# A two-layer hybrid decoder step: sums of squares, a group mean and modulation products regrouped on TensorE

## The chip, the cores and the metric

The kernel runs on one core of a Trainium2 chip. The metric is the device time of one execution in microseconds; lower is better. The traces are of single profiled executions.

## What is computed

Two decoder layers are applied to a prompt of 512 tokens and to 8 samples of 4 tokens (32 tokens), so activations are 1024 channels by 544 tokens. Cut to what the change touches:

```python
mod = silu(c) @ w_ada + b_ada            # 9 conditioning vectors, 1024 -> 6*1024
h   = rmsnorm(x, norm1) * (1 + sc1) + sh1
q   = rope(rmsnorm(q per head of 64, q_norm), pos)     # 16 heads
k   = rope(rmsnorm(k per head of 64, k_norm), pos)     # 4 heads
...
# state-space branch, 4 groups of 512 channels
y, hT = ssd_scan(xs, dt, A, B, C, h0)    # h0: one state of 512 x 128 per sample and group
yg = y * silu(z), in 4 groups
yg = yg * rsqrt(mean(yg * yg, over the group's 512 channels) + eps)
```

Everything is float32. The large projections are split in a high and a low float32r half of both operands, so one projection tile is three products.

## The kernel before

Channels lie on partitions, tokens on the free axis: an activation of 1024 channels is 8 tiles of 128x544. `gemm` (L336) multiplies one weight block of 1024x128 with the 8 tiles of `h`: 8 x 3 weights x 2 halves of 272 tokens, 48 products, of which the trace mostly shows rows of two (x2). A weight block comes by DMA on SP's queue into `raw` (four buffers, L318), ScalarE makes its high half `wh` (L177), VectorE its low half `wl` (L322), with three buffers of each.

Side work is written as Python generators in four lanes. Each `gemm` first advances each lane by its rate (`pump`). Lane "c" holds the state-space chains, in the order in which they are pushed, lane "a" the modulation, lanes "s" and "t" the indexer's scores and its top-k. A scheduler in the compiler then sorts each engine's instructions by priorities and by times of its own; the order is fixed before the run, and each engine takes its instructions strictly in that order.

The places that the change touches:

- **Modulation** (`ada`). A call makes 16 blocks of 128 columns. Per call there are four accumulators, each 128x512, and four loads of `raw` (128x1024, L250) per accumulator. Each load feeds two products (L253): 32 columns of stationary conditioning vectors, 512 moving columns. A product writes one of four bands of 32 partitions: the first and third load write bands 0 and 1, the second and fourth write bands 2 and 3. There is a `yield` behind each load, so a `gemm` stands between two loads' products. Six calls in all: the first in the prologue, two during layer 0's pooling and attention, three during layer 0's feed-forward part.
- **Sums of squares** (`ssq`, L483), for 8 query tiles and 2 key tiles per layer. The squared tile is the stationary operand, in five blocks of tokens; two columns of 1/64 are the moving one. The rsqrt is three Newton steps on VectorE (L271 to L276) on 128x80 (queries) or 128x20 (keys).
- **The state-space mean** (`norm_rows`), once per group, 8 in all. Five products with one column (L284) put the mean with tokens on partitions, Newton runs on 128x5 elements, five products with the identity (L295, L297) spread the result over all partitions, and ScalarE copies it to `rb`. L1137 multiplies `Y` by `rb`; `oh` and `ol` (L310) are its halves, which the next product of the branch takes (L336, `psg<-oh,wh`).
- **States of the samples** (`ssd_sample`). Per group, 8 states `h0` (128x512; the trace strips the digit and says `h`) are loaded four at a time (L1084), and a `yield` later each is multiplied by 32 columns of `cm` into one of four bands (L1088).

In float32 the trace shows two records for a product of TensorE (a float32r product and a transpose have one). L740 (`kx`, indexer keys of the samples) is another product in four bands of 32.

## Time and profile before

| | |
|---|---|
| median of 3 runs | 3217.64 us (3216.38 to 3218.22) |
| profiled execution: time, span | 3219.4 us, 3217.6 us |
| busy in the span: TensorE, VectorE, ScalarE, GpSimd | 3117.6 (97%), 2229.4 (69%), 1258.1 (39%), 892.9 us (28%) |
| mean granted clock of TensorE | 0.985 of full speed |

The time of an execution is the span from the first to the last recorded instruction and 1.8 us around it. Busy time of TensorE counts overlapping products once. In the views below a row of the timeline is one or more equal instructions in a row, with its start and its length; the distance from its start to the next row's start is what it took on an engine that is never idle.

### The profile page before, as it was taken

To read this page: it belongs to the slowest core of one execution; us is meant where nothing else is said; L and a number is where in the kernel's file an instruction comes from. 1 tells how busy PE (TensorE), PEld (TensorE's weight loads), DVE (VectorE), ACT (ScalarE), POOL (GpSimd) and SP (SyncE) were. 2 spreads that over 40 slices of the span, in tenths; PEclk is the share of its full clock that TensorE was granted. 3 is DMA by queue.
4 is the path that set the end of the run, shared out by engine and by line. 5 is a ranking of instruction groups with operands and counts; after the bars stand their busy time and mean duration, and the time that the engine had idled before them with its cause. 6 is when DMAs were issued, how large, how long until landed. Compare 5 with 4: busy or idle time off the path is not lost. (4 is left out here: it accounts for less than half of the span.)

```text
span 3217.6 us, 63012 instructions
## 1 busy us (share of the span) xinstructions
PE 3117.6 (97%) x24322; PEld 2834.3 (88%) x24322; DVE 2229.4 (69%) x4827; ACT 1258.1 (39%) x2228; POOL 892.9 (28%) x1271
## 2 busy tenths in 40 slices
PE   7999999999999999999999999999999999999999
PEld 5987898999896788888989978989999967899999
DVE  5687788679878655444566877886799976564554
ACT  4344443333236534333443444433342365352432
POOL 2373445421021002111223544455120210030211
PEclk8999999999999999999999999999999999999999
DMA  6332332345433434445334323233233234333322
GB/s 231 104 104 77 110 95 101 105 151 179 164 117 129 157 133 115 147 146 147 105 104 122 98 82 106 89 96 119 95 129 117 91 125 154 106 84 94 78 98 78
DMA packets 303102, 376.85 MB, mean 117 GB/s; under 512 B 177362, under 2 KB 186930, under 8 KB 302802
## 3 DMA queue, kind: packets, MB, share of 16 engines
q1 hardware_dynamic: 116514, 315.94, 29.3%
q10 hardware_dynamic: 181216, 42.05, 6.4%
q0 software_dynamic: 5072, 14.83, 1.2%
q8 instruction: 192, 3.15, 0.4%
q14 instruction: 108, 0.88, 0.1%
HBM read 330.34 MB, written 33.79 MB: 113 GB/s over the span
## 5 line engine op out<-in xcount | busy, mean ns | idle before, releaser
L177 ACT ACTIVATE wh<-raw 128x1024 fp32r<-128x1024 f32 (+2 forms) x434 | 424.9, 980 | 1199.7 <-PE psg L336 909.6
L336 PE MATMUL psg<-hh,wh 128*128 128x272 f32 x4064 | 863.7, 292 | 7.8 <-ACT cacc L839 5.4
L336 PE MATMUL psg<-hl,wh 128*128 128x272 f32 x4064 | 856.0, 290 | 0.0
L336 PE MATMUL psg<-hh,wl 128*128 128x272 f32 x4064 | 853.6, 290 | 0.0
L322 DVE TENSOR_TENSOR wl<-raw,wh 128x1024 fp32r<-128x1024 f32 (+2 forms) x434 | 510.5, 1176 | 354.1 <-ACT wh L177 349.8
L336 PEld LDWEIGHTS psg<-hh,wh 128*128 128x128 f32 x4064 | 642.6, 189 | 61.9 <-issue 28.1
L336 PEld LDWEIGHTS psg<-hh,wl 128*128 128x128 f32 x4064 | 643.9, 189 | 17.1 <-issue 15.3
L336 PEld LDWEIGHTS psg<-hl,wh 128*128 128x128 f32 x4064 | 644.1, 189 | 15.9 <-issue 14.4
L841 POOL COPY sti<-cu 128x32 f32<-128x32 f32 x136 | 91.3, 672 | 588.9 <-ACT cu L177 588.6
L846 DVE SCALAR_TENSOR_TENSOR cacc<-cu,half,cacc 128x511 f32<-128x511 f32 x144 | 134.9, 937 | 6.8 <-ACT cacc L839 6.3
L336 PE MATMUL psg<-fh,wh 128*128 128x272 f32 x648 | 135.4, 291 | 2.6 <-DVE resid L460 2.6
L855 ACT ACTIVATE th<-cacc 128x544 f32<-128x544 f32 x92 | 60.5, 657 | 196.1 <-DVE cacc L849 187.5
L454 DVE SCALAR_TENSOR_TENSOR x<-psg,mod,x 128x272 f32<-128x272 f32 x64 | 32.0, 500 | 151.6 <-PE psg L336 142.6
L336 PE MATMUL psg<-fl,wh 128*128 128x272 f32 x648 | 133.7, 287 | 0.0
L336 PE MATMUL psg<-fh,wl 128*128 128x272 f32 x648 | 133.7, 288 | 0.0
L336 PEld LDWEIGHTS psg<-fh,wh 128*128 128x128 f32 x648 | 101.2, 188 | 14.3 <-issue 6.7
L336 PE MATMUL psg<-oh,wh 128*128 128x272 f32 x512 | 110.4, 294 | 0.0
L336 PE MATMUL psg<-ol,wh 128*128 128x272 f32 x512 | 109.5, 291 | 0.0
L336 PE MATMUL psg<-oh,wl 128*128 128x272 f32 x512 | 109.0, 292 | 0.0
L856 DVE SCALAR_TENSOR_TENSOR cacc<-th,cacc 128x544 f32<-128x544 f32 x92 | 71.3, 775 | 49.2 <-ACT th L855 49.0
L986 POOL TENSOR_TENSOR seg<-seg,cb 128x512 f32<-128x512 f32 x64 | 88.9, 1392 | 54.3 <-ACT seg L985 46.8
L336 PEld LDWEIGHTS psg<-fl,wh 128*128 128x128 f32 x648 | 101.7, 188 | 0.0
(469 smaller groups left out, 6232.4 us busy)
## 6 DMA issues: line engine op xcount, KB each, us to landing
raw<-wk SPq DMA_DIRECT2D x326, 512.0 KB, 3.5
raw<-w_ada SPq DMA_DIRECT2D x96, 512.0 KB, 3.5
h<-h SPq DMA_DIRECT2D x64, 256.0 KB, 3.8
raw<-wk SPq DMA_DIRECT2D x64, 256.0 KB, 2.8
o_ssds<-hn ACTq DMA_DIRECT2D x64, 256.0 KB, 2.2
raw<-wd SPq DMA_DIRECT2D x32, 448.0 KB, 3.4
kvr<-ckv SPq DMA_DIRECT2D x48, 256.0 KB, 3.6
kvw<-ckv SPq DMA_DIRECT2D x48, 256.0 KB, 4.0
```

Of the source, the lines that this page charges most:

```text
L177: self.nc.scalar.activation(out, src, AF.Copy)
L322: self.last_wl = self.E("weights1").tensor_tensor(wl[:, :n], raw[:, :n], wh[:, :n].bitcast(F32), op=OP.subtract).ins
L336: nc.tensor.matmul(o[:, c, :HC], w[:, k * 128:(k + 1) * 128], x[:, c * HC:(c + 1) * HC], start=(k == 0 and first), stop=(k == K - 1 and last))
L454: self.E("resid1").scalar_tensor_tensor(x[:, :HC], o[:, 0, :HC], g[:, 0:1], x[:, :HC], op0=OP.mult, op1=OP.add)
L841: self.E("conv1").tensor_copy(st[:, i, :, W - 1:], new)
L846: self.E("conv3").scalar_tensor_tensor(acc[:, s:512], u[:, :512 - s], wc, acc[:, s:512], op0=OP.mult, op1=OP.add)
L855: nc.scalar.activation(th, acc, AF.Tanh)
L856: self.E("silu21").scalar_tensor_tensor(acc, th, 1.0, acc, op0=OP.add, op1=OP.mult)
L986: self.E("ssd_chain5").tensor_tensor(d[:, :512], d[:, :512], cb[:, :512], op=OP.mult)
```

## The change

Four edits.

- **Modulation.** The loads are taken in pairs: the first of a pair is followed by a `yield`, then both loads' four products are written back to back, one in each band.
- **Sums of squares.** A block of 128x32 (`blk32`, the two columns of 1/64 and 30 of zeros) is now stationary and the squared tile moves (512 and 32 columns). Four query tiles, or two key tiles, go to four (two) bands. ScalarE copies the bands out, TensorE transposes them back. The Newton steps of the queries run per four tiles on 128x40. `qsq` leaves the tag "R" (one buffer) for "T" (49 buffers).
- **The state-space mean.** One 128x128 stationary block of 1/512 gives the mean on all partitions (512 and 32 moving columns). The Newton steps run on 128x544. The five products with the identity and the copies to `rb` are gone.
- **States of the samples.** The first four loads of `h0` stand at the head of `ssd_sample`, the second four behind the first four products, and the `yield` between loads and products is gone.

```diff
 def ada(...):
         for c in range(4):
             ps = self.P("ada1")
-            for z in range(4):
-                i = 4 * c + z
-                with self.tc.high_priority(offset=WPRI):
-                    raw = self.wr.tile([128, 1024], F32, name="raw", tag="raw")
-                    nc.sync.dma_start(raw, a["w_ada"][l, s, i])
-                for q in range(2):
-                    k, g = 2 * z + q, 32 * (2 * (z % 2) + q)
-                    nc.tensor.matmul(ps[g:g + 32, :], self.sc[:, k, :], raw[:, q * 512:(q + 1) * 512],
-                                     start=(k < 4), stop=(k >= 4))
-                if z < 3:
+            for pair in range(2):
+                raws = []
+                for z in (2 * pair, 2 * pair + 1):
+                    with self.tc.high_priority(offset=WPRI):
+                        raw = self.wr.tile([128, 1024], F32, name="raw", tag="raw")
+                        nc.sync.dma_start(raw, a["w_ada"][l, s, 4 * c + z])
+                    raws.append(raw)
+                    if z % 2 == 0:
+                        yield
+
+                for k4 in range(4):
+                    nc.tensor.matmul(ps[32 * k4:32 * k4 + 32, :], self.sc[:, 4 * pair + k4, :],
+                                     raws[k4 // 2][:, (k4 % 2) * 512:(k4 % 2) * 512 + 512],
+                                     start=(pair == 0), stop=(pair == 1))
+                if pair == 0:
                     yield
...
 def norm_rows(self, sq, wcol, eps, out):
-        ps = self.P("norm_rows1")
-        for i in range(5):
-            w = 128 if i < 4 else 32
-            nc.tensor.matmul(ps[:w, i:i + 1], sq[:, i * 128:i * 128 + w], self.mean_w[:, wcol:wcol + 1],
-                             start=True, stop=True)
...
+        o, o2 = self.P("norm_rows1"), self.P("norm_rows2")
+        nc.tensor.matmul(o, self.mean512, sq[:, :512], start=True, stop=True)
+        nc.tensor.matmul(o2[:, :32], self.mean512, sq[:, 512:], start=True, stop=True)
+        m, u, y = self.t("nrm"), self.t("nru"), self.t("rb")
+        nc.vector.tensor_scalar(m[:, :512], o, eps, None, op0=OP.add)
+        nc.vector.tensor_scalar(m[:, 512:], o2[:, :32], eps, None, op0=OP.add)
+        yield
+        self.newton(m, u, y)
+        out.append(y)
         yield
...
-    def ssq(self, sq, ps, c0):
-        for i in range(5):
-            w = 128 if i < 4 else 32
-            self.nc.tensor.matmul(ps[:w, i * 16 + c0:i * 16 + c0 + 2], sq[:, i * 128:i * 128 + w], self.blk,
-                                  start=True, stop=True)
+    def ssq(self, sqs, name):
+
+        nc, n = self.nc, len(sqs)
+        o, o2 = self.P("ssq3"), self.P("ssq4")
+        for z, sq in enumerate(sqs):
+            nc.tensor.matmul(o[32 * z:32 * z + 32, :], self.blk32, sq[:, :512], start=True, stop=True)
+        for z, sq in enumerate(sqs):
+            nc.tensor.matmul(o2[32 * z:32 * z + 32, :32], self.blk32, sq[:, 512:], start=True, stop=True)
+        rows = self.t("ssr")
+        self.copy("ssq1", rows[:32 * n, :512], o[:32 * n])
+        self.copy("ssq1", rows[:32 * n, 512:], o2[:32 * n, :32])
...
+        for i in range(4):
+            nc.tensor.transpose(ps[:, 128 * i:128 * i + 32 * n], rows[:32 * n, 128 * i:128 * i + 128],
+                                self.ident[:32 * n, :32 * n])
...
 def ssd_sample(self, q):
+        def states(hf):
+            h0s = [self.t("h0") for z in range(4)]
+            for z in range(4):
+                nc.sync.dma_start(h0s[z][:, :512], a["h0"][l, g, 4 * hf + z])
+            return h0s
+        nxt = states(0)
...
-            h0s = [self.t("h0") for z in range(4)]
-            for z in range(4):
-                nc.sync.dma_start(h0s[z][:, :512], a["h0"][l, g, 4 * hf + z])
-            yield
+            h0s = nxt
             for z in range(4):
...
-            if hf:
+            if not hf:
+                nxt = states(1)
+            else:
...
 def attention(self):
         for i in range(8):
...
-            self.ssq(sq, ps, 2 * i)
+            sqs.append(sq)
+            if i % 4 == 3:
+                mk = self.ssq(sqs, "mq")
+                self.newton(mk, self.s([128, 5, 8], "rsq_u8"), rq[:, :, 2 * i - 6:2 * i + 2])
+                sqs = []
```

What the diff alone does not show is how the scheduler places the products. A row below is a line, an operation, output and inputs, the output's shape and a count; the lines after L216 are shifted in the changed program (gemm L336 is L339, modulation L253 is L263, states L1088 is L1109, `kx` L740 is L757).

On TensorE in layer 0's feed-forward part, before: two loads (`raw_15524`, `raw_15593`) with one gemm (output `psg_15534`) between them.

```order
L253 MATMUL psb_15523<-raw_15524,sc_101 32x512 x2
L336 MATMUL psg_15534<-hh_14969,wh_15530 128x272 x2
L336 MATMUL psg_15534<-hl_14977,wh_15530 128x272 x2
...
L336 MATMUL psg_15534<-hh_14976,wl_15531 128x272 x2
L253 MATMUL psb_15523<-raw_15593,sc_101 32x512 x2
L336 MATMUL psg_15603<-hh_14969,wh_15599 128x272 x2
```

The same place in the changed program:

```order
L339 MATMUL psg_15505<-hh_14949,wl_15502 128x272 x2
L263 MATMUL psb_15496<-raw_15497,sc_106 32x512 x2
L263 MATMUL psb_15496<-raw_15564,sc_106 32x512 x2
L339 MATMUL psg_15576<-hh_14942,wh_15572 128x272 x2
...
L339 MATMUL psg_15651<-hh_14949,wl_15648 128x272 x2
L263 MATMUL psb_15496<-raw_15643,sc_106 32x512 x2
L263 MATMUL psb_15496<-raw_15710,sc_106 32x512 x2
```

Two loads' products now stand together, with two gemms to the next four. Counted over the program without the prologue (its 32 products stand as before), the 160 modulation products stood in 71 uninterrupted runs (61 of two, 7 of four, one each of one, three and six) and now stand in 44 (35 of four, 5 of two, 2 of one, one each of three and five).

On TensorE in layer 0's first state-space group, before: the second four states of the samples (`h0_2731` to `h0_2734`).

```order
L1088 MATMUL psa_2606<-h0_2731,cm_2603 32x512
L745 MATMUL psb_2636<-rel_2634,wsel_1588 32x512
L336 MATMUL psg_3005<-hh_145,wl_3002 128x272 x2
L1088 MATMUL psa_2606<-h0_2732,cm_2603 32x512
L336 MATMUL psg_3005<-hh_146,wh_3001 128x272 x2
L336 MATMUL psg_3005<-hl_154,wh_3001 128x272 x2
L336 MATMUL psg_3005<-hh_146,wl_3002 128x272
L1088 MATMUL psa_2606<-h0_2733,cm_2603 32x512
```

The same group in the changed program (`h0_2494` on are the first four, `h0_2633` on the second):

```order
L1109 MATMUL psa_2624<-h0_2494,cm_2621 32x512
L1091 MATMUL psb_2612<-smt_2525,sxdt_2507 64x32 x8
L1109 MATMUL psa_2624<-h0_2495,cm_2621 32x512
L1109 MATMUL psa_2624<-h0_2496,cm_2621 32x512
L1109 MATMUL psa_2624<-h0_2497,cm_2621 32x512
...
L1109 MATMUL psa_2624<-h0_2633,cm_2621 32x512
L1109 MATMUL psa_2624<-h0_2634,cm_2621 32x512
L1109 MATMUL psa_2624<-h0_2635,cm_2621 32x512
L1109 MATMUL psa_2624<-h0_2636,cm_2621 32x512
```

The states that stood one by one between gemm products now stand together. Over the program, the 64 state products stood in 40 runs (30 of one, 6 of three, 4 of four) and now stand in 18 (4 of one, 4 of three, 8 of four, 2 of eight); the 32 products of L740 go from 10 runs to 8 of four. The 20 sums of squares of 512 columns do not all stand together: 10 stand alone and 10 in 5 pairs, each as soon as its tile is there, so 15 runs, and the 20 of 32 columns likewise, mostly right behind them.

On VectorE in layer 0's second state-space group the changed program has, from the mean (`nrm`) to the product with `Y` (the Newton steps are L286 to L291, L325 makes `wl`):

```order
L301 TENSOR_SCALAR nrm<-psa 128x512
L302 TENSOR_SCALAR nrm<-psa 128x32
L795 TENSOR_TENSOR qs<-qi,qs 64x384
L286 TENSOR_SCALAR nru<-nrm 128x544
L325 TENSOR_TENSOR wl<-raw,wh 128x512
L287 TENSOR_SCALAR rb<-nru 128x544
L919 SCALAR_TENSOR_TENSOR zt<-zt,psg 128x544
L289 TENSOR_TENSOR nru<-rb 128x544
L290 SCALAR_TENSOR_TENSOR nru<-nru,nrm 128x544
L291 SCALAR_TENSOR_TENSOR rb<-nru,rb 128x544
...
L1160 SCALAR_TENSOR_TENSOR Y<-Y,par,rb 128x544 x4
```

Left out are the second and third Newton step and one more `wl` of 128x512. Before, the same eleven instructions of the Newton steps were on 128x5. On TensorE, between the mean's two products and the first product that takes `oh`, this group's changed program has 58 gemm products and 4 indexer products of 256 and 384 columns; in the third group it is nearly twice that work, in the others more. In SP's order the loads of `h0` stand where they stood, or within a few entries of it; only those of each layer's first group moved, 15 to 25 entries ahead.

## Rows read from the trace of the kernel before

**Rows 1.** The page: TensorE's busy time and granted clock (tenths, 40 slices).

```profile
PE 3117.6 (97%) x24322; PEld 2834.3 (88%) x24322; DVE 2229.4 (69%) x4827; ACT 1258.1 (39%) x2228; POOL 892.9 (28%) x1271
...
PEclk8999999999999999999999999999999999999999
```

**Rows 2.** Instruction groups by form: count, busy us and mean ns, idle before.

```profile
L253 PE MATMUL psb<-raw,sc 128*32 128x512 f32 x384 | 92.7, 636 | 1.6 <-DMA raw<-w_ada 1.6
```

**Rows 3.** Timeline of TensorE: start, length, line, count of records.

```profile
217.22 1.06 PE L1088 MATMUL psa<-h,cm 128*32 128x512 f32 x8
218.22 1.06 PE L740 MATMUL psa<-kx,qis 64*32 64x512 f32 x8
...
228.12 1.04 PE L1088 MATMUL psa<-h,cm 128*32 128x512 f32 x2
229.09 0.39 PE L336 MATMUL psg<-hh,wl 128*128 128x272 f32 x1
...
803.16 0.41 PE L336 MATMUL psg<-hl,wh 128*128 128x272 f32 x2
803.41 0.41 PE L336 MATMUL psg<-hh,wl 128*128 128x272 f32 x2
803.75 1.05 PE L253 MATMUL psb<-raw,sc 128*32 128x512 f32 x4
804.74 0.52 PE L336 MATMUL psg<-ph,wh 128*128 128x272 f32 x2
805.09 0.41 PE L336 MATMUL psg<-pl,wh 128*128 128x272 f32 x2
```

**Rows 4.** Timeline of TensorE at the mean of the second group.

```profile
393.54 1.10 PE L284 MATMUL psa<-mean_w,sqy 128*128 128x1 f32 x10
394.57 0.38 PE L783 MATMUL psa<-ikh,qs 128*128 128x256 f32 x1
...
403.59 1.05 PE L295 MATMUL psa<-cst,rstd 128*128 128x128 f32 x8
404.57 0.40 PE L297 MATMUL psa<-cst,rstd 32*128 32x32 f32 x2
404.91 0.52 PE L336 MATMUL psg<-hl,wh 128*128 128x272 f32 x2
...
410.64 0.41 PE L336 MATMUL psg<-oh,wh 128*128 128x272 f32 x2
```

**Rows 5.** Timeline of TensorE: sums of squares of a query tile, narrow products, transposes (by form).

```profile
874.73 1.10 PE L483 MATMUL psb<-cst,qsq 128*128 128x2 f32 x10
875.76 0.39 PE L336 MATMUL psg<-hh,wl 128*128 128x272 f32 x1
...
286.24 0.24 PE L757 MATMUL psa<-ki,qis 64*32 64x4 f32 x8
286.41 0.52 PE L336 MATMUL psg<-oh,wh 128*128 128x272 f32 x2
...
L965 PE MATMUL psa<-cst,cacc 128*128 128x128 f32 x128 | 20.0, 279 | 0.0
```

**Rows 6.** VectorE and ScalarE in the second group (timeline), and prices by form.

```profile
405.40 2.87 DVE L1137 SCALAR_TENSOR_TENSOR Y<-Y,par,rb 128x544 f32<-128x544 f32 x4 [1.62 <-ACT rb L177]
...
406.22 1.36 ACT L177 ACTIVATE oh<-Y 128x544 fp32r<-128x544 f32 x2 [0.85 <-DVE Y L1137]
...
L1381 DVE TENSOR_SCALAR S<-S,asm 128x512 f32<-128x512 f32 x32 | 15.5, 484 | 0.6
```

**Rows 7.** Loads by size with us to landing (page); SP and TensorE, feed-forward part (timeline).

```profile
raw<-w_ada SPq DMA_DIRECT2D x96, 512.0 KB, 3.5
...
1280.19 0.33 SPq L250 DMA_DIRECT2D raw<-w_ada  x1
...
1279.10 1.05 PE L253 MATMUL psb<-raw,sc 128*32 128x512 f32 x4
...
1294.38 1.05 PE L253 MATMUL psb<-raw,sc 128*32 128x512 f32 x4
```

More of the change, by code (lines that the diff above doesn't have):

```diff
@@ L210, in consts @@
         nc.vector.memset(self.mean_w[:, 1:2], 1.0 / 512)
+        self.blk32 = self.cp.tile([128, 32], F32, name="blk32")
+        nc.vector.memset(self.blk32, 0.0)
+        nc.vector.tensor_copy(self.blk32[:, 0:2], c[:, C_BLK:C_BLK + 2])
+        self.mean512 = self.cp.tile([128, 128], F32, name="mean512")
+        nc.vector.memset(self.mean512, 1.0 / 512)
         self.selc = self.cp.tile([128, 32], F32R, name="selc")
@@ L269, in rsqrt, with newton @@
         u = self.s(shape, "rsq_u%d" % shape[-1], bufs=2)
+        return self.newton(m, u, y)
+    def newton(self, m, u, y):
+        nc = self.nc
         mi, yi, ui = m.bitcast(I32), y.bitcast(I32), u.bitcast(I32)
@@ L478, in rope_tables @@
         self.nc.scalar.dma_start(self.sin, self.a["cossin"][1])
-    def ssq(self, sq, ps, c0):
-        for i in range(5):
-            w = 128 if i < 4 else 32
-            self.nc.tensor.matmul(ps[:w, i * 16 + c0:i * 16 + c0 + 2], sq[:, i * 128:i * 128 + w], self.blk,
-                                  start=True, stop=True)
+    def ssq(self, sqs, name):
[8 more added lines that the diff above has]
+        self.copy("ssq1", rows[:32 * n, 512:], o2[:32 * n, :32])
+        mk = self.s([128, 5, 2 * n], name)
+        nc.gpsimd.memset(mk, 1.0)
+        ps = self.P("ssq1")
+        for i in range(4):
+            nc.tensor.transpose(ps[:, 128 * i:128 * i + 32 * n], rows[:32 * n, 128 * i:128 * i + 128],
+                                self.ident[:32 * n, :32 * n])
+        pv = ps.rearrange("p (i z c) -> p i z c", i=4, z=4)
+        mv = mk.rearrange("p i (z c) -> p i z c", c=2)
+        nc.vector.tensor_scalar(mv[:, 0:4], pv[:, :, :n, 0:2], EPS, None, op0=OP.add)
+        ps = self.P("ssq2")
+        nc.tensor.transpose(ps[:32, :32 * n], rows[:32 * n, 512:], self.ident[:32 * n, :32 * n])
+        pv = ps[:32, :128].rearrange("p (z c) -> p z c", z=4)
+        nc.vector.tensor_scalar(mv[:32, 4], pv[:, :n, 0:2], EPS, None, op0=OP.add)
+        return mk
     def layer(self, l):
@@ L580, in k_chain @@
         kt = [self.t("kt0"), self.t("kt1")]
-        ps = self.P("k_chain1")
+        mk = self.ssq([raws[p][1] for p in range(2)], "mk")
         for p in range(2):
-            self.ssq(raws[p][1], ps, 2 * p)
             self.rope(raws[p][0], kt[p])
             yield
-        mk = self.s([128, 5, 4], "mk", bufs=1)
-        pv = ps[:, :80].rearrange("p (i c) -> p i c", c=16)
-        nc.gpsimd.memset(mk, 1.0)
-        self.E("k_chain1").tensor_scalar(mk[:, 0:4], pv[:, 0:4, 0:4], EPS, None, op0=OP.add)
-        self.E("k_chain2").tensor_scalar(mk[:32, 4], pv[:32, 4, 0:4], EPS, None, op0=OP.add)
         rk = self.rsqrt(mk, [128, 5, 4], "rk")
@@ L1289, in attention @@
             filler()
-        mk = self.s([128, 5, 16], "mq")
-        pv = ps[:, :80].rearrange("p (i c) -> p i c", c=16)
-        nc.gpsimd.memset(mk, 1.0)
-        self.E("attention3").tensor_scalar(mk[:, 0:4], pv[:, 0:4], EPS, None, op0=OP.add)
-        self.E("attention4").tensor_scalar(mk[:32, 4], pv[:32, 4], EPS, None, op0=OP.add)
-        rq = self.rsqrt(mk, [128, 5, 16], "rq")
         sq8 = self.s([128, 4, 16], "sq8")
```

21 lines of the change are left out of this document (3 added, 18 removed).

## The prediction

> **What bounds the kernel.** I read the page first: TensorE is busy for 3117.6 of 3217.6 us, at 0.8 of full speed in the first fortieth and full speed after it, and VectorE for 2229.4 [rows 1]. So 100 us of TensorE's span are waits, and every microsecond of work taken off TensorE comes back as time, as long as nothing that TensorE waits for becomes later. The second view is TensorE's timeline, read by the distance between starts, because lengths overlap: two gemm products take 0.25 us (803.16 to 803.41). What is to be seen in it is the price of a product with 32 stationary columns [rows 3]. Four of them, in four bands, take 1.00 us (217.22 to 218.22). Two modulation products in two bands take 0.99 us (803.75 to 804.74). One state product alone takes 0.97 us (228.12 to 229.09). So what counts is not products but uninterrupted runs of up to four. A run also makes its neighbours longer: the gemm row ahead of one takes 0.34 us (803.41 to 803.75), the one behind it 0.35 us (804.74 to 805.09), where 0.25 is usual. That is 0.99 + 0.09 + 0.10 = 1.18 us per run. The profiled execution took 3219.4 us, 1.8 us over its span; the median is 3217.64, so I make the sum against the span, put the 1.8 us back, and take the 1.8 us off again for the median: in effect the difference is taken from 3217.6.
>
> **Modulation products.** Outside the prologue, whose order does not change, 71 runs become 44, as counted from both orders. That is 27 runs at 1.18 us; the one run of five takes half a run more, the one of six before it did too, and the two cancel: -31.9 us. I take -31.4, because some runs border on other packed work and pay no second border. What it depends on is the second load of a pair. Today a load is issued at 1280.19, right behind the products that free its buffer (1279.10 plus 1.05); with two of four buffers holding modulation blocks it is used at 1294.38, 14 us later [rows 7], and all modulation products together waited 1.6 us for a load [rows 2]. A run of four now frees two buffers at once. The next weight load takes one of them, and its gemm stands two gemms (48 products, 6 us each) and another run later, 13 us; it lands in 3.5 us [rows 7], which leaves 9 us for its two casts. The modulation load behind it on SP is used later still. I therefore take 0 for new waits, with 1 us per run (+44 us) as the upper end, should the weights behind a blocked modulation load on SP come late.
>
> **The samples' states.** 40 runs become 18, of which the two of eight take a run's length more: 22 x 1.18 - 2 x 1.0 = -24 us. The products of L740 lose two runs: -2.4 us. The earlier loads add nothing to the traffic; in SP's order most stand where they did, so nothing is queued behind them that was not before; those of each layer's first group stand 15 to 25 entries ahead.
>
> **The mean of a group.** Before, the five products with one column take 1.03 us (393.54 to 394.57), those with the identity 0.98 and 0.34 us (403.59 to 404.91), and each of the two stretches lengthens its border by about 0.10 us as above: 2.55 us per group [rows 4]. After, one product of 512 columns with 128 stationary columns: no row has it in float32. Four products of 128 columns take 0.98 us [rows 4], which is the same number of columns, and I take that; the single product with 32 stationary columns, 0.97, says the same. The narrow one costs at most the 0.34 us of the 32-column one before. With a border, 1.4 us per group, so 8 x 1.15 = -9.1 us.
>
> **Sums of squares.** Before, 20 tiles at 1.03 us (874.73 to 875.76) [rows 5] and 18 borders of 0.10: 22.4 us. After, the scheduler does not keep four tiles together: 15 runs of 512 columns at 0.98, as many of 32 columns, bounded by 0.17 us for a packed run of four very narrow products (286.24 to 286.41) and by 0.34 above, at 0.17 as the nearest; six sets of transposes, 20.0 us over 32 sets of four, 0.62 us [rows 5]; and 0.2 us of borders for each of the 15 runs: 14.7 + 2.6 + 3.7 + 3.0 = 24.0. That is +1.6 us; with 0.34 for the narrow ones it is +4, without their borders -1.4. So this edit alone should give nothing on TensorE, and the sum would be the same without it. Its copies (12 on ScalarE, where 16 copies to `rb` go) and its smaller Newton steps lie beside gemms.
>
> **Newton steps on 544 columns.** This is what the change adds. VectorE's operations with two tensor operands take 0.72 us for 128x544 (2.87 for four) [rows 6]. A group has nine of them, three with one operand, for which I take the 0.48 us of the row for 512 columns, also for the two integer ones, which no row has at this width, and a short one: 9 x 0.72 + 3 x 0.48 + 0.2 = 8.1 us, 65 us over the eight groups, of VectorE's 988 us of idle time [rows 1]. Most of it lies under gemms. It is on TensorE's path only where the product with `oh` comes too soon. Before, in the second group, 17.1 us pass from the sum to that product (393.54 to 410.64) [rows 4], and `oh` is made from 406.22 on [rows 6]. In the changed order of that group TensorE has the mean (1.3 us), 58 gemm products (7.3 us) and four short ones (0.6 us), 9.2 us. VectorE has the 8.1 us and, between them, two `wl` of 512 columns, one `zt` and one `qs`, 2.4 us at about 0.6 each; with the mean ahead of it (1.3), the first `Y` and `oh` behind it (0.7 + 0.7) and some 0.3 for hand-overs that is 13.5 us. So TensorE stands for about 4 us, in each layer. The third group has nearly twice that work on TensorE, 16 us, and some 16 us in its chain, since more of others' instructions stand in it; I take 0. The first and fourth have 20 us or more. Sum +8 us; the bounds are 5 (operations at 0.57 us) and 16 (the third group late by 4 us too).
>
> **The sum.** -31.4 - 24 - 2.4 - 9.1 + 1.6 + 8 = -57.3 us: 3160 us, 1.8% less. TensorE's own work is down by 65 us, and 8 us of waits are new.
>
> **A rule to weigh.** The rows show four products in four bands for 1.00 us against 0.97 us for one [rows 3]. The Trainium skill (TensorE: Matmul & The Clock Gate, "Part 3: Packing small matmuls — row/col tiling") gives a measured gain of 3.07 for four row tiles and 2.38 for three column tiles, less than the number of tiles. By 3.07, a run of four would cost 1.30 singles, 1.27 us here, and the 47 runs of four that the modulation and the states have (two of eight counted twice) would give back 14 us: 3174 by the page. By the row it is 3160, and I take the row, which is this kernel's own.
>
> **Rivals.**
> - *Packing gives less.* A run of four lies a third of the way from one run's length to two, 1.29 us, in all 47 of them (+15 us), and 20 more borders than I count split the gemms (+4): 3179. Against it: the four-band runs of 1.00 us stand beside the same gemms.
> - *The loads come late.* The run of four waits for its second load, or the weights queued behind a blocked modulation load come late, 0.7 to 1 us in each of 44 runs, 31 to 44 us: 3191 to 3204. For it: today's pair frees one buffer at a time. Against it: the 14 us of lead [rows 7].
> - *Newton's steps hold TensorE in every group: not faster, or slower.* The place is the first `oh` product of a group. The wait would have to reach 65/8 = 8.1 us per group to cancel the gain; the whole chain is 13.5 us, so no more than 5.4 us of gemms could lie beside it. With 12 us standing in each group it is 3217.6 - 65 + 96 = 3249. For it speaks that `oh` needs all of the chain; against it, that the order has 9 us beside it in the second group and 16 and more in the others.
> - *The sums of squares really stand four together in time,* or fewer interruptions shorten more than the borders that I count, 8 to 15 us more: 3145 to 3152.
>
> **The numbers.** Chances: the forecast (3152 to 3170) 0.56; packing gives less 0.15; loads late 0.10; gains larger 0.13; Newton's steps hold TensorE 0.06, of which half is slower. The likeliest is 3160. The range reaches from 3144 to 3186: it leaves out the late loads, the Newton case and the far end of the larger gains, under 2 in 10. A difference under 0.2% (6.4 us) can't be told from none here. The Newton case is half same and half slower: faster 0.94, same 0.03, slower 0.03.
>
> **What would show it.** In the profile after: TensorE's busy time near 3053 us; modulation near 64 us (27 runs fewer) after 92.7 [rows 2]; the state products' runs of four at 1.0 us; the mean's two products at 1.3 us per group; sums of squares that together are no cheaper than before; VectorE's busy time up by 40 to 65 us; and a wait of TensorE for `oh` of some 4 us in the second group of each layer. Wrong I would be if the runs of four took well over 1.0 us, if waits for `raw` or `wh` appeared by the tens of microseconds, or if waits for `oh` came in all groups.

## The result and the profile after

The changed kernel takes 3190.53 us (median of 4 executions, 3189.45 to 3195.12), the kernel before beside it 3217.93. The ratio is 0.9911, interval 0.9893 to 0.9930: 28 us less, where 57 were forecast, and outside the range. The profiled execution has a span of 3189.4 us, 28.2 less than before.

The page of the changed kernel, busy times and TensorE's granted clock, answers to [rows 1]:

```profile
PE 3051.6 (96%) x24104; PEld 2800.3 (88%) x24104; DVE 2271.8 (71%) x4856; ACT 1258.1 (39%) x2224; POOL 887.4 (28%) x1265
...
PEclk9998999999999999999989989999999999999999
```

TensorE's busy time fell by 66.0 us; 65 were forecast. But its idle time, span less busy, rose from 100.0 to 137.8 us: +38 where +8 was forecast. So the total of TensorE's work went as the sum said, in part by luck, as the stretches below show; its waits did not. VectorE's busy time rose by 42 us, inside the 40 to 65 that were forecast.

Where the waits are is read from the windows of the two state-space stretches, one per layer, from the first gemm products of the branch to the first product of the pooling (columns: window, its length, busy time of each engine with its instructions, granted clock, DMA share, GB/s):

```profile
147.00:704.90 557.90, 528.27 (x4062) 482.43 (x4060) 451.08 (x837) 210.41 (x365) 258.46 (x294) 0.97 0.32 101
1746.10:2305.80 559.70, 532.11 (x4110) 490.39 (x4109) 453.72 (x848) 214.63 (x370) 261.33 (x295) 0.97 0.31 98
sum 1117.60, PE 1060.38 PEld 972.82 DVE 904.80 ACT 425.04 POOL 519.79; mean PE 530.19 PEld 486.41 DVE 452.40 ACT 212.52 POOL 259.90
```

Before, the same stretches (147.0 to 699.1 and 1774.7 to 2329.4; granted clock 0.99 and 0.98) have the line of sums

```profile
sum 1106.80, PE 1082.61 PEld 979.92 DVE 860.58 ACT 431.04 POOL 515.67; mean PE 541.30 PEld 489.96 DVE 430.29 ACT 215.52 POOL 257.84
```

TensorE has 22 us less to do there, waits 33 us more (57.2 against 24.2), and the stretches are 11 us longer, where the sum had them 27.5 shorter (-24, -2.4, -9.1 and +8). The rest of the span is 39 us shorter, against 29.8 in the sum. All that is missing is missing in the state-space stretches. Busy time there fell by 22 us where the sum had 35.5, and in the rest by 44 where it had 29.8: that the total came out right is in part luck.

TensorE's waits in the changed kernel (line, releaser: total, times, longest) name two that the list of before does not have (there another product waits 1.4 us for `cb`, once per layer):

```profile
PE psg L339 <- ACT oh L177: 17.3, 4, 7.0
PE psa L982 <- DVE cb L970: 14.4, 2, 7.2
```

The first is the one that was forecast, at 4 us in the second group of each layer; it is 7.0 there, and 1.0 and 2.2 in the third groups, where 0 was forecast. The timeline around the second group's mean shows it (TensorE and then VectorE; answers to [rows 4] and [rows 6]):

```profile
398.41 1.13 PE L298 MATMUL psa<-sqy,mean 128*128 128x512 f32 x2
399.38 0.30 PE L299 MATMUL psa<-sqy,mean 128*128 128x32 f32 x2
399.52 0.50 PE L339 MATMUL psg<-hl,wh 128*128 128x272 f32 x2
...
407.18 0.41 PE L339 MATMUL psg<-hh,wl 128*128 128x272 f32 x2
414.61 0.82 PE L339 MATMUL psg<-oh,wh 128*128 128x272 f32 x2 [7.03 <-ACT oh L177]
415.23 0.63 PE L800 MATMUL psa<-ikh,qs 128*128 128x512 f32 x1
415.66 0.63 PE L801 MATMUL psa<-ikl,qs 128*128 128x512 f32 x1
416.08 1.91 PE L959 MATMUL psa<-cacc 128*128 128x128 f32 x8
417.65 0.80 PE L339 MATMUL psg<-ol,wh 128*128 128x272 f32 x2
...
397.66 2.04 DVE L863 SCALAR_TENSOR_TENSOR cacc<-cu,half,cacc 128x511 f32<-128x511 f32 x2
...
401.75 0.72 DVE L873 SCALAR_TENSOR_TENSOR cacc<-th,cacc 128x544 f32<-128x544 f32 x1 [0.79 <-ACT th L872]
402.39 0.68 DVE L301 TENSOR_SCALAR nrm<-psa 128x512 f32<-128x512 f32 x1
...
405.74 0.72 DVE L289 TENSOR_TENSOR nru<-rb 128x544 f32<-128x544 f32 x1
406.49 0.72 DVE L290 SCALAR_TENSOR_TENSOR nru<-nru,nrm 128x544 f32<-128x544 f32 x1
...
413.09 2.87 DVE L1160 SCALAR_TENSOR_TENSOR Y<-Y,par,rb 128x544 f32<-128x544 f32 x4
```

The mean is done at 399.5. VectorE is in the convolution (`cacc`) until 402.39 and only then adds eps (L301); from there to `Y` it needs 10.7 us. TensorE's gemm products end at 407.6, as forecast, and `oh` is ready at 414.61.

The second wait was not in the sum. It is in the first group of each layer (VectorE, then TensorE):

```profile
255.35 0.72 DVE L291 SCALAR_TENSOR_TENSOR rb<-nru,rb 128x544 f32<-128x544 f32 x1
...
257.32 2.87 DVE L1160 SCALAR_TENSOR_TENSOR Y<-Y,par,rb 128x544 f32<-128x544 f32 x4
260.11 2.63 DVE L313 TENSOR_TENSOR ol<-Y,oh 128x544 fp32r<-128x544 f32 x4
262.65 0.69 DVE L960 TENSOR_TENSOR cb<-psa,cst 128x512 f32<-128x512 f32 x1
...
263.48 1.08 PE L982 MATMUL psa<-cst,cacc 128*128 128x128 f32 x4 [7.21 <-DVE cb L970]
...
266.96 2.69 PE L757 MATMUL psa<-kx,qis 64*32 64x512 f32 x8 [0.81 <-ACT ecs L1001]
269.58 1.12 PE L982 MATMUL psa<-cst,cacc 128*128 128x128 f32 x4
```

`cb` belongs to the next group. It reads a PSUM buffer, and stands on VectorE behind the Newton steps, four `Y` and four `ol` of this group; the transposes of L982 wait for it. The steps do not make all of this wait: without the new mean it is 4.0 us, as the experiments show.

Both waits cost more than their length. The eight records of L757 stand 2.62 us from the next row (266.96 to 269.58), where such a run takes 1.00 at full speed [rows 3]. The windows, with the granted clock third from the end, show most of the reason. The first is the second group's wait, the second the work behind it, the third the work behind the wait for `cb`:

```profile
407.60:414.60 7.00, 0.00 (x0) 0.00 (x0) 6.79 (x11) 1.61 (x4) 0.97 (x3) 0.65 0.15 53
414.60:420.04 5.44, 5.43 (x22) 5.23 (x23) 5.44 (x10) 4.03 (x8) 0.00 (x0) 0.50 0.00 0
263.50:270.00 6.50, 5.33 (x16) 2.40 (x17) 2.76 (x9) 2.44 (x5) 3.54 (x3) 0.50 0.01 3
```

The clock falls while TensorE waits, and the products behind each wait run at 0.50, which is 1.2 GHz instead of 2.4, for 5 us and more. Ahead of the wait (398.4 to 407.6) it was 1.00.

Modulation went as forecast. Its group of instructions, by form, answers to [rows 2]:

```profile
L263 PE MATMUL psb<-raw,sc 128*32 128x512 f32 x384 | 65.1, 642 | 2.3 <-DMA raw<-w_ada 2.3
```

65.1 us after 92.7, against 64 forecast, and 2.3 us of waits for loads after 1.6, so the loads that [rows 7] follow stayed in time. In TensorE's timeline one run, four products as eight records, takes 0.99 us between two gemm rows (answers to [rows 3]), and behind another such run stand the sums of squares of two query tiles, which the scheduler split as expected, in 1.02 us with their narrow products, where [rows 5] had 1.03 for one tile:

```profile
1231.26 0.41 PE L339 MATMUL psg<-hh,wl 128*128 128x272 f32 x2
1231.61 1.06 PE L263 MATMUL psb<-raw,sc 128*32 128x512 f32 x8
1232.60 0.52 PE L339 MATMUL psg<-hh,wh 128*128 128x272 f32 x2
1232.96 0.41 PE L339 MATMUL psg<-hl,wh 128*128 128x272 f32 x2
...
873.76 1.03 PE L488 MATMUL psa<-qsq,blk 128*32 128x512 f32 x4
874.62 0.23 PE L490 MATMUL psa<-qsq,blk 128*32 128x32 f32 x2
874.78 0.52 PE L339 MATMUL psg<-hh,wh 128*128 128x272 f32 x2
```

### The profile page after: what moved, and what is told of

The parts are those of the page before. It is cut to its first block, busy times and chain, and to the rows that moved or that the text cites. A ratio compares the mean times of both kernels' runs of the same rounds, so it can differ in the third digit from the quotient of the medians.

```text
span 3189.4 us, 62617 instructions
## 1 busy us (share of the span) xinstructions
PE 3051.6 (96%) x24104; PEld 2800.3 (88%) x24104; DVE 2271.8 (71%) x4856; ACT 1258.1 (39%) x2224; POOL 887.4 (28%) x1265
## 4 chain that ended last, share of the span: by engine, by line
PE 80%; DVE 8%; issue 3%; DMA 3%; ACT 2%; POOL 1%; ACTq 1%; SPq 0%; DVEq 0%; POOLq 0%
PE psg L339 62%; PE psg L356 2%; DMA raw<-wk 1%; PE psb L1023 1%; PE psb L263 1%; DVE wl L325 1%; PE psb L1418 1%; PE psa L582 1%; PE psb L1009 1%; ACT wh L177 1%; PE psb L1032 1%; DVE cacc L866 1%; PE psa L1413 1%; DMA kvr<-ckv 1%; PE psg L1390 1%
## 5 line engine op out<-in xcount | busy, mean ns | idle before, releaser
L339 PE MATMUL psg<-hh,wh 128*128 128x272 f32 x4064 | 856.1, 291 | 8.1 <-ACT cacc L856 5.8
L339 PE MATMUL psg<-hl,wh 128*128 128x272 f32 x4064 | 850.8, 289 | 0.0
L339 PE MATMUL psg<-hh,wl 128*128 128x272 f32 x4064 | 849.0, 289 | 0.0
L325 DVE TENSOR_TENSOR wl<-raw,wh 128x1024 fp32r<-128x1024 f32 (+2 forms) x434 | 511.9, 1179 | 305.4 <-ACT wh L177 304.1
L339 PEld LDWEIGHTS psg<-hh,wh 128*128 128x128 f32 x4064 | 640.4, 189 | 38.9 <-issue 13.9
L339 PEld LDWEIGHTS psg<-hh,wl 128*128 128x128 f32 x4064 | 640.1, 189 | 9.1 <-issue 7.5
L339 PEld LDWEIGHTS psg<-hl,wh 128*128 128x128 f32 x4064 | 639.7, 189 | 7.5 <-issue 6.5
L858 POOL COPY sti<-cu 128x32 f32<-128x32 f32 x136 | 82.6, 607 | 546.7 <-ACT cu L177 539.8
L339 PE MATMUL psg<-fh,wh 128*128 128x272 f32 x648 | 134.8, 290 | 2.6 <-DVE resid L463 2.6
L339 PE MATMUL psg<-oh,wh 128*128 128x272 f32 x512 | 113.4, 301 | 22.3 <-ACT oh L177 17.3
L339 PE MATMUL psg<-fl,wh 128*128 128x272 f32 x648 | 133.7, 288 | 0.0
L339 PE MATMUL psg<-fh,wl 128*128 128x272 f32 x648 | 133.6, 288 | 0.0
L339 PE MATMUL psg<-ol,wh 128*128 128x272 f32 x512 | 112.7, 298 | 1.2 <-DVE ol L313 1.2
L339 PE MATMUL psg<-oh,wl 128*128 128x272 f32 x512 | 112.0, 297 | 0.0
L339 PEld LDWEIGHTS psg<-fh,wh 128*128 128x128 f32 x648 | 100.9, 188 | 10.1 <-issue 4.2
L339 PEld LDWEIGHTS psg<-oh,wh 128*128 128x128 f32 x512 | 84.4, 196 | 27.8 <-ACT oh L177 18.2
L1595 POOL TENSOR_TENSOR cacc<-cacc 128x544 f32<-128x544 f32 x44 | 61.1, 1388 | 156.4 <-DVE cacc L873 150.5
```

Source lines behind the costliest of these rows:

```text
L325: self.last_wl = self.E("weights1").tensor_tensor(wl[:, :n], raw[:, :n], wh[:, :n].bitcast(F32), op=OP.subtract).ins
L339: nc.tensor.matmul(o[:, c, :HC], w[:, k * 128:(k + 1) * 128], x[:, c * HC:(c + 1) * HC], start=(k == 0 and first), stop=(k == K - 1 and last))
L858: self.E("conv1").tensor_copy(st[:, i, :, W - 1:], new)
L1595: self.E("ffn3").tensor_tensor(s_, s_, aa, op=OP.mult)
```

## The experiments

Theory A: the Newton steps on 128x544 hold VectorE; the next group's work behind them comes late, TensorE waits and falls to the lower clock. Theory B, the rival: the early start of the states and the new order of the stretch cost the time.

### Each part by itself

Four kernels are the kernel before with one part of the change (`norm_rows`; `ssd_sample`; `ada`; `ssq` with its two callers), one is the changed kernel without its new mean, and one has modulation and states only.

> The changed kernel with the group's mean made as before: five narrow products, three Newton steps on 128x5, spread by a transpose; all other parts of the change stay. Theory A (the Newton steps on 128x544 hold TensorE up in the first and second group of each layer and the clock falls behind those waits) expects 3160 to 3170 us: the 18.8 us of narrow products come back, and some 38 us of idle time and half-clock products go. Theory B (the early start of the states and the new order of the state-space stretch cost it, the mean itself saves its 9 us) expects 3195 to 3205 us, slower than the changed kernel.

> The kernel before with the new mean alone (one product, Newton steps on 128x544). Theory A expects it slower than before by 10 to 25 us (3228 to 3243 us). Theory B expects it faster by 1 to 9 us (3209 to 3217 us).

> The kernel before with the states fetched half a group earlier and their four products placed in one run, nothing else. Theory A expects the forecast's 24 us and the 2 us of L740's products, 3191 to 3200 us. Theory B expects no gain or a loss, 3212 to 3230 us.

> The kernel before with the modulation's products four at once, nothing else. Both theories expect the forecast's 31 us, 3182 to 3190 us, since the milestones outside the state-space stretches moved by about 32 us.

> The kernel before with the sums of squares alone: four tiles at once, copied out, transposed back, and the query tiles' squares in the large pool of buffers. The forecast had this part at +1.6 us by the scheduler's splits; the products' own sum over the line in the changed kernel gives about -4. Both expect 3212 to 3222 us. The rival expects that it is this part that takes back some 10 us of what modulation (32 us) and states (12 us) give each by itself, since the two and this one together gave 34: 3224 to 3232 us.

> The kernel before with modulation and states, without the sums of squares and with the old mean. If the parts add up, 31 and 12 us: 3172 to 3180 us. If the two get into each other's way, as the 34 us of the kernel with the old mean and the squares would have it, 3183 to 3190 us.

| kernel | median us | ratio to before, interval | forecast of this part |
|---|---|---|---|
| modulation alone | 3189.84 | 0.9905 (0.9888 to 0.9922) | -31.4 us: 0.990 |
| states alone | 3210.36 | 0.9961 (0.9950 to 0.9972) | -26.4 us: 0.992 |
| squares alone | 3222.51 | 1.0002 (0.9989 to 1.0016) | +1.6 us: 1.000 |
| mean alone | 3236.68 | 1.0048 (1.0030 to 1.0065) | -1.1 us: 1.000 |
| all but the mean | 3188.35 | 0.9893 (0.9870 to 0.9916) | |
| modulation and states | 3181.34 | 0.9874 (0.9858 to 0.9891) | |

By the ratios the four parts measure -31, -13, +1 and +15 us (in the order of the table): together -28, which is what the whole change gives. Modulation and squares are as forecast. The mean alone makes the kernel slower, as theory A has it, and the states give half of their forecast, which is between the theories. Without the mean the kernel should then be at -43; modulation and states are at -41 (3181.34 us, 1 us above what a plain sum was expected to give), and with the squares the middle is -34, with an interval that reaches from -27 to -42. The kernel without the mean met neither A's 3160 to 3170 us nor B's 3195 to 3205, and it is only 6 us faster than the whole change, with intervals that overlap: by medians, taking the wide steps out of the whole change gives little. Its trace shows where the difference goes. Its state-space stretches are 15.6 us shorter than the changed kernel's,

```profile
sum 1102.00, PE 1066.38 PEld 977.52 DVE 856.01 ACT 429.39 POOL 508.96; mean PE 533.19 PEld 488.76 DVE 428.00 ACT 214.69 POOL 254.48
```

with 0.8 us of waits for `oh` instead of 17.3 and 4.0 us at `cb` instead of 7.2 in each layer, so there theory A holds. The rest of its span is 14 us longer, 9 of them behind the second stretch, where the two kernels have the same code. In the traces of all kernels that last part takes from 882 to 892 us; why is not known. A difference of a few us between two traces, here or below, is therefore weak evidence.

In the kernel with the mean alone the waits are the two of the changed kernel:

```profile
PE psa L963 <- DVE cb L951: 15.2, 2, 8.0
...
PE psg L334 <- ACT oh L177: 12.7, 4, 4.1
```

Its windows of the state-space stretches (the line of sums) show that TensorE's saving is gone:

```profile
sum 1129.10, PE 1077.42 PEld 976.33 DVE 902.48 ACT 427.41 POOL 521.78; mean PE 538.71 PEld 488.17 DVE 451.24 ACT 213.70 POOL 260.89
```

TensorE is busy for 5 us less than the 1082.61 of before, waits for 51.7 us instead of 24.2, and the stretches are 22 us longer. Measured from start to start and summed over the rows of both stretches, the mean's products went from 18.8 to 8.0 us, as forecast; the gemm products, without the waits ahead of the next row, went from 804 to 814, though their number is the same. That is the lower clock: 0.97 granted in both stretches, where before had 0.99 and 0.98.

With the states alone TensorE waits for VectorE at three places more:

```profile
PE psa L965 <- DVE cb L953: 8.0, 2, 4.0
PE psg L336 <- DVE ol L310: 6.0, 4, 1.7
...
PE psg L336 <- DVE zt L902: 4.7, 4, 1.3
```

and its windows' sum is

```profile
sum 1100.70, PE 1067.98 PEld 979.75 DVE 858.15 ACT 429.51 POOL 514.53; mean PE 533.99 PEld 489.87 DVE 429.08 ACT 214.76 POOL 257.27
```

The products of `h` went from 41.5 to 21.5 us in 20 runs instead of 40 (from start to start), so their price was right. TensorE's busy time fell by 14.6 us in the stretches, and its idle time rose by 8.5 (from 24.2 to 32.7): the waits for `cb`, `ol` and `zt` are more than the older ones that went. No wide step is in this kernel.

### Is it the gemm products that stand between the mean and oh?

In TensorE's order the gemm products between mean and first `oh` product (the cover) number 116, 97, 114 and 126 in the four groups of layer 0 before, 118, 58, 111 and 154 after, and 118, 58, 45 and 171 with the states alone. Theory C was that these covers, shortened by the scheduler, are what costs; D, its rival, that the states' early fetch itself does. The number of steps that a gemm advances the chains shifts the covers:

```
-        self.lane("c", 4)
+        self.lane("c", 7)
```

and in two more kernels four steps in groups 0 and 1 and seven in groups 2 and 3, which leaves the first group alone.

> The kernel before with one number changed: the lane of the groups' chains is advanced seven steps at each gemm of the state-space stretch instead of four. In TensorE's order the gemm products between a group's mean and the first product of oh then number 96, 84, 45 and 149 in the four groups, where the kernel before has 116, 97, 114 and 126 and the kernel with the states alone has 118, 58, 45 and 171. Theory C (cover: the wait ahead of oh depends on how many gemm products the scheduler leaves between mean and oh; the states' lost 12 us are such waits) expects the waits of the kernel with the states alone, some 3 us in the third group of each layer and 1 us in the second, so 5 to 12 us slower than before (3223 to 3230 us). Its rival D (the early fetch of the states itself holds the stretch up, by its buffers or its DMA) expects no difference from before beyond 3 us.

> The kernel before with the states' part of the change alone, at seven steps instead of four: 112, 106, 105 and 154 gemm products stand between mean and oh. Theory C expects the idle time ahead of oh to go and the full forecast of this part, 22 to 28 us (3190 to 3196 us). Rival D expects what four steps gave, 12 us (3203 to 3210 us).

> The changed kernel with the mean as before, at seven steps: modulation, sums of squares and states, with 112, 106, 105 and 154 products of cover. Theory C expects 3158 to 3170 us (31 us of modulation and 24 to 26 us of states, the sums of squares near nothing); rival D expects 3180 to 3190 us, as at four steps.

> The whole change at seven steps: 112, 106, 113 and 154 products of cover instead of 118, 58, 111 and 154. Theory A (the wide Newton steps, about 12 us of VectorE behind other work, reach past a cover of some 60 products but less past one of over 100) with C expects the 7.0 us wait of the second group to fall to 2 to 4 us and the time to 3172 to 3184 us, still slower than the same kernel with the old mean. The rival (the wide Newton steps hurt by filling VectorE, not by their place) expects no change from 3190 us.

> The changed kernel with the mean as before, and the lane of the chains advanced four steps per gemm in the first two groups and seven in the last two. Products between mean and oh: 118, 106, 105 and 154, where four steps throughout give 118, 58, 45 and 171; the first group stays as it was. Theory C (cover) expects the waits ahead of oh in the second and third group to go and oh of the fourth group to come 6 to 10 us earlier in each layer: 3170 to 3178 us. Its rival (the lost 12 us of the states are slower products at other places, not waits ahead of oh) expects 3185 to 3192 us, no difference.

> The whole change with the same two rates: 118, 106, 113 and 154 products between mean and oh, where four steps have 118, 58, 111 and 154. Theory A with C expects the wait of the second group (7.0 us) to fall under 2.5 us and the time to 3172 to 3182 us, the first group's wait behind cb staying at 7 us. The rival (only the length of the steps on VectorE counts, not what covers them) expects 3187 to 3194 us.

| seven steps | ratio, interval | at four steps |
|---|---|---|
| before | 1.0062 (1.0043 to 1.0080) | 1 |
| states alone | 0.9999 (0.9988 to 1.0010) | 0.9961 |
| all but the mean | 0.9944 (0.9927 to 0.9960) | 0.9893 |
| whole change | 0.9910 (0.9891 to 0.9929) | 0.9911 |
| all but the mean, 4 4 7 7 | 0.9897 (0.9873 to 0.9922) | 0.9893 |
| whole change, 4 4 7 7 | 0.9906 (0.9876 to 0.9935) | 0.9911 |

C missed in all six. D missed too in the first three; in the other three the time was as the rivals expected, none of which gives the cover a part. Seven steps cost the kernel before 20 us, more than C had, with a wait of 11.4 us in all for `cb`; with the covers long again the states are no faster than the kernel before at four steps. Against the kernel before at seven steps, though, they give 20 of the 26 us forecast. With 4 4 7 7 the whole change has the longer cover, and TensorE's waits for `oh` fall from 17.3 to 8.7 us; but its waits for `cacc` (L339 behind the convolution) grow from 6.5 to 10.1, and the time is not told apart from the changed kernel's. So more gemm products as cover moved a wait to another place and gave no time. That seven steps leave the whole change where it is and cost the other kernels 12 to 20 us is not explained. It limits theory A: at seven steps the kernel with the wide mean is, by ratios, 11 us faster than the one with the old mean (the intervals barely touch), so what the wide steps cost holds for the order at four steps and not for any order.

### The length of the Newton steps

One step instead of three in `newton` for the mean (two are left out); a buffer of its own for the result; and the same three steps on a quarter of the columns, which needs four products to spread the result:

```
+        for z in range(4):
+            nc.tensor.matmul(o[32 * z:32 * z + 32, :W], self.mean512[:, :32], sq[:, W * z:W * z + W], ...)
+        nc.vector.tensor_scalar(m, o[:, :W], eps, None, op0=OP.add)          # 128x136, W = 136
+        self.newton(m, u, y)
+        for z in range(4):
+            ps = o[:, W * z:W * z + W] if z < 3 else o2[:, :W]
+            nc.tensor.matmul(ps, self.ident[:, 32 * z:32 * z + 1].to_broadcast([128, 128]), y, ...)
+        self.copy("norm_rows3", rb[:, :3 * W], o[:, :3 * W])
+        self.copy("norm_rows4", rb[:, 3 * W:], o2[:, :W])
```

> The whole change with one Newton step instead of three in the group's mean (two steps are left out, so the mean's root is coarse): six operations of 0.75 us fewer on VectorE for each group, the cover as in the changed kernel (122, 58, 113 and 170 products). Theory A expects the second group's wait to fall from 7.0 to about 2.5 us and the first group's behind cb from 7.2 to about 2.7 us, with part of the half-clock stretches behind them: 3160 to 3176 us. The rival (the wide steps are hidden, what costs is the new order) expects 3186 to 3192 us.

> The whole change with one name altered: the result of the Newton steps takes a buffer of the large pool instead of the single one that it shares with xdt and yq. TensorE's order between mean and oh is as in the changed kernel (118, 58, 111 and 154 gemm products). Theory A expects no difference, 3186 to 3194 us, the 7 us waits staying. The rival (the single buffer is held through the steps, and xdt or yq of the next group wait for it) expects 3165 to 3180 us.

> The whole change, but the group's mean is made by four products with 32 columns side by side (tokens 136 z to 136 z + 135 on partitions 32 z to 32 z + 31), the three Newton steps run on 128x136 instead of 128x544, and four products with one-hot columns and two copies on ScalarE spread the result. Nothing is left out. Theory A (what costs is the time that the wide steps hold VectorE) expects at least what one step instead of three gave, 3165 to 3180 us, with the second group's 7 us wait and the first group's wait behind cb mostly gone. If the new place of the mean costs, and not the steps, 3187 to 3196 us.

> The kernel before with the group's mean alone, by four products of 32 columns side by side, Newton steps on 128x136 and four spreading products; nothing is left out. Theory A expects the products' saving, 18.8 us of old products against 3 to 4 us and 8 us, so 7 us, with no new idle time: 3208 to 3215 us. If any new form of the mean costs waits here, 3220 us or more.

One step: 3175.69 us, ratio 0.9854 (0.9828 to 0.9881), as theory A expected. Waits for `oh` fall from 17.3 to 3.9 us (longest 2.0; 2.5 was expected), those for `cb` from 7.2 to 1.7 each (2.7 expected). A buffer of its own: 3200.34 us, 0.9940 (0.9924 to 0.9957), no gain, so the shared buffer is not the cause; but three of its four executions took 3200 to 3205 us, longer than theory A's 3186 to 3194, which is not explained. Its profiled execution, 3187.79 us, has the same 7.0 and 7.2 us waits. Quarter-width steps: 3167.82 us, 0.9832 (0.9816 to 0.9849), as theory A expected, faster than the kernel before and the changed one by intervals that don't meet, with nothing left out. The timeline of its second group, VectorE and TensorE:

```profile
394.31 0.29 DVE L302 TENSOR_SCALAR nrm<-psa 128x136 f32<-128x136 f32 x1
...
400.32 0.30 DVE L291 SCALAR_TENSOR_TENSOR nry<-nru,nry 128x136 f32<-128x136 f32 x1
...
402.39 2.87 DVE L1169 SCALAR_TENSOR_TENSOR Y<-Y,par,rb 128x544 f32<-128x544 f32 x4 [1.17 <-ACT rb L177]
...
391.84 0.44 PE L299 MATMUL psa<-sqy,mean 128*32 128x136 f32 x8 [0.42 <-POOL sqy L1162]
...
400.68 1.19 PE L309 MATMUL psa<-nry,cst 128*128 128x136 f32 x8 [0.98 <-DVE nry L291]
...
403.78 1.05 PE L968 MATMUL psa<-cacc 128*128 128x128 f32 x8
404.59 0.85 PE L348 MATMUL psg<-oh,wh 128*128 128x272 f32 x4
```

The sum of its windows over the two stretches:

```profile
sum 1094.20, PE 1055.86 PEld 966.02 DVE 865.26 ACT 429.84 POOL 517.47; mean PE 527.93 PEld 483.01 DVE 432.63 ACT 214.92 POOL 258.73
```

An operation takes 0.30 us instead of 0.72, and the product with `oh` starts without a wait. VectorE has 40 us less to do than in the changed kernel, TensorE 5 less, and the stretches are 23 us shorter, at a granted clock of 0.99 and 0.98 instead of 0.97. That bears theory A out. Not all waits went: those for `oh` fell from 17.3 to 1.0 us, but `cb` still holds TensorE,

```profile
PE psa L991 <- DVE cb L979: 10.3, 2, 5.2
```

and the idle time in the stretches is 38.3 us, against 57.2 in the changed kernel and 24.2 before. Nor is it the width alone that differs: spreading adds products and copies, and the scheduler leaves 45 instead of 111 gemm products ahead of `oh` in the third group.

On the kernel before, the quarter-width mean alone gives 3219.27 us, 0.9995 (0.9986 to 1.0005): the 15 us of loss are gone, but the 7 us that its products save were expected and did not come. The windows show TensorE busy for 1065.4 of 1101.7 us: 17 less to do, 12 more of waits. Of these, 8 are again at `cb`: L747 (`kx`) waits 5.4 us in each layer, where before had 1.4. The profile names no releaser here, but in both layers the product starts 0.1 us behind the end of the 512-column `cb` on VectorE, so it is taken here for the same wait.

### The states' two halves

The states' part does two things: it fetches half a group earlier, and it drops one `yield` ahead of the products. One kernel keeps the `yield`; one has only the dropped `yield` (a line less in the kernel before).

> The kernel before with the states' early fetch, but with the step of the lane ahead of their products kept, which the change dropped. If the dropped step is what takes back half of the states' gain, 3191 to 3198 us; if the early fetch and the faster products themselves do (TensorE saves 20 us and then waits for VectorE and GpSimd in the third and fourth group), 3204 to 3212 us, as without the step.

> The kernel before with one step of the lane dropped ahead of the states' products (one line), the fetch as before. If the dropped step alone carries the states' 12 us, 3203 to 3211 us; if it does so only where the fetch is early, so that the products stand in one run, 3214 to 3224 us, with the products of h in some 40 runs.

Early fetch with the `yield`: 3218.76 us, 0.9994 (0.9984 to 1.0003); no gain, less than either of the two expectations, though the products of `h` stand in 22 runs and take 23.5 us. The dropped `yield` alone: 3226.71 us, 1.0012 (0.9998 to 1.0027); no gain, 42 runs. Only together do they give 13 us. In the windows the first has TensorE 11 us less busy and 16 us more idle. Which instruction of the order makes the difference was not found.

One wait is common to these kernels, though, with wide steps or without: TensorE behind `cb` of the next group, in the first group of each layer. Before it is 1.4 us; with the early fetch alone 3.8 (again without a named releaser, 0.1 us behind `cb`), with the dropped `yield` alone 5.1, with both 4.0, before at seven steps 5.7, with the quarter-width mean alone 5.4, with the wide mean alone 8.0 and in the whole change 7.2. So a mere shift of the order can bring this wait out. The traces do not show that it accounts for all that was lost.

## Why the prediction was wrong

**Modulation** was right: -31 us measured alone (-25 to -36), -31.4 forecast, by a run of four at 0.99 us. By the Trainium skill (TensorE: Matmul & The Clock Gate, "Part 3: Packing small matmuls — row/col tiling") four row tiles gain 3.07; the 35 runs of four would then each be 0.28 us longer, an estimate of 10 us less gain, some 21. The trace does not agree with that figure for these products, which stand side by side in four bands of the output (four take 0.99 us, one 0.97), and the measured interval leaves it out.

**Sums of squares** were right: nothing, within 0.16%.

**Newton steps on 544 columns** is the step that failed first. The sum had +8 us, between 5 and 16. Measured alone, the mean with them is at +15 us (+10 to +21) instead of -1. The price of an operation, 0.72 us, was right. Wrong were three things in the traces. The chain was taken to start when the mean is done; it started 3 us later, behind the convolution, so the second group's wait was 7.0 instead of 4. The first group was given "20 us or more" of cover, since I looked for the wait at `oh` alone; it came at `cb`, an instruction of the next group, queued on VectorE behind the steps, 7.2 us in each layer, of which 3.2 come with the steps and 4.0 stand there without the new mean too. And a wait was priced at its length, while the products after it ran in part at 1.2 GHz: 10 us over the gemm products, with the mean alone. The sum had no term for the clock; the digits of [rows 1] were read as full speed, but a 9 there means 90% or more. The quarter-width steps show it from the other side: with them 25 us come back (0.9911 less 0.9832). With the old mean only 6 come back, though its stretches are 15.6 us shorter.

**The samples' states** are the second. The products cost nearly what the sum said (20 us saved of 24, and those of L740 0.8 of 2.4), but "every microsecond of work taken off TensorE comes back as time, as long as nothing that TensorE waits for becomes later" was taken into the sum without a price for its condition, and in the state-space stretches the condition does not hold. With the states alone, in layer 0, TensorE comes 1.1 us earlier than before to the place where it waits for `cb`, and the 512-column `cb` ends 1.4 us later. In the stretches of one trace each, 14.6 us less work gave 6 us with the states alone, 17 gave 5 with the quarter-width mean alone, and 11 gave nothing with the early fetch alone: the rest is new idle time of TensorE, part of it at `cb`. By medians the states gave 13 us of 26.4. The 100 us of idle time on the page said that waits are few; it didn't say how close behind TensorE the chains of the other engines stand there. In the pooling, attention and feed-forward stretches, where modulation's products are, the sentence held.

**The rival** "Newton's steps hold TensorE in every group" had the right mechanism at 0.06; its price, 12 us in each group, was too high, and its place, `oh`, was half of it. The time that was measured lies just short of another rival's, the late loads (3191 to 3204 us), whose mechanism did not happen: modulation waited 2.3 us for loads.

Left open: why the early fetch pays only with the dropped step, why seven steps per gemm cost some kernels 12 to 20 us and the whole change nothing, and why the part of the span behind the second stretch differs by up to 10 us between traces of kernels with the same code there.

## What to carry to other kernels

TensorE at 97% busy is an average: before crediting work taken off it, ask in the stretch where it lies which engine runs just behind TensorE, at which instruction TensorE would next wait for it, and what share of the saving would only become idle time. Work added to an in-order engine is priced by everything queued behind it, the next stage's first instructions too, not by the one consumer that it feeds. A value that all partitions share can be computed on a quarter of the columns, with tokens split over four bands of partitions, and spread afterwards: here two-operand steps fell from 0.72 to 0.30 us.

## What the hardware showed that I had not expected

- A wait of 7 us leaves TensorE slow behind it: from 414.61 to 420.04, behind 7.03 us without work, the granted clock is 0.50; the eight transposes of L959 take 1.57 us from start to next start, and 0.81 in the kernel with quarter-width steps (403.78 to 404.59), where no wait ahead of them is longer than 1 us and the clock is 1.00.
- Four float32 products of 136 columns in four bands take 0.44 us as one row (391.84), and the spreading ones, 128 columns stationary, 1.19.
